# Feature-major products with high and low activations side by side as 512 moving columns, in groups of 512 outputs

## The chip, the cores and the metric

The kernel runs on one core of a Trainium2 chip. The metric is the device time of one execution in microseconds (us), given as the median of several runs. The profile is one further execution, taken by the hardware profiler; in it PE is TensorE's matmuls, PEld its weight loads, DVE VectorE, ACT ScalarE, POOL GpSimd, and SP the engine that issues nearly all DMAs.

## What is computed

A decoder trunk of two layers on one sequence of 256 tokens with 2048 features, in float32. Each layer is a token mixer and a gated MLP, each behind an RMSNorm that is shifted, scaled and gated by vectors made from a conditioning vector `c`:

```python
cond = silu(c)
for i in range(2):
    sh_m, sc_m, g_m, sh_f, sc_f, g_f = split(cond @ w_mod[i] + b_mod[i], 6)     # w_mod[i]: 2048 x 12288
    h = rmsnorm(x, norm_mix[i]) * (1 + sc_m) + sh_m
    y = gla_mixer(h, ...) if i == 0 else fox_mixer(h, ...)
    x = x + (1 + g_m) * y
    h = rmsnorm(x, norm_ffn[i]) * (1 + sc_f) + sh_f
    u = causal_depthwise_conv3(h @ w_up[i]) + conv_b[i]                         # w_up[i]: 2048 x 11264
    x = x + (1 + g_f) * ((silu(u[:, :5632]) * u[:, 5632:]) @ w_down[i])         # w_down[i]: 5632 x 2048
out = rmsnorm(x, norm_final)
```

The first mixer is chunked gated linear attention (input product 2048 x 6160 for q, k, v, a gate r and a rank-16 forget gate a; output product 2048 x 2048). The second is softmax attention with a cumulative forget-gate bias (input product 2048 x 8208 for q, k, v, an output gate and 16 forget logits; output product 2048 x 2048).

## The kernel before

**Numbers.** The large products are float32 products made of three fp32r matmuls. A weight tile `w` (128 rows by 1024 columns) is split into `wh` (a cast to fp32r on ACT, L110) and `wl = w - wh` (a subtraction on DVE, L111). The activations are split in the same way into a high part `rh` and a low part `rl`, which lie in one SBUF tile of shape [128, 2, 4, 256] (high and low parts of four row tiles). The product is wh·rh + wh·rl + wl·rh; the fourth term is left out.

**Streaming.** All weights pass once through the core, in the order of one list, `plan`: 816 tiles of 128 x 1024 (512 KB each) and three narrow ones. `next_w` loads them into a ring of five SBUF buffers (`RING`) and splits them up to three tiles ahead (`AHEAD`); the split halves have four buffers each. The same ring also holds the tiles `wm` of `w_mod`: the modulation vectors are background work, one 128 x 1024 tile at a time, multiplied by a column of silu(c) and added up on DVE (`acc`, L248). `tick`, called after each weight tile, loads and runs this background work and a queue of small steps (`side`: convolution, attention, operand preparation) at rates set by hand for each stage (`pace`, `set_pace`).

**Feature-major products, `stream_a`.** A weight tile gives eight output tiles of 128 features by 256 tokens (m = 0 to 7). For each, three matmuls with 256 moving columns are issued: wh with rh (L540), wh with rl (L541), wl with rh (L542), each with its own weight load. Four PSUM banks hold the eight outputs, two to a bank, and each row tile k of the contraction is added on. PSUM has eight banks: a pool `psA` of six (`PS[0]`), from which each product takes four, so that two are free when the next product begins, and a pool `psM` of two for all small work. The same pool serves the transposes that finish the modulation vectors (`pt`, L261) when they are wide or deferred.

The products of this form are: q, k and r of the linear attention (in two halves of the contraction, `BLOCKS`), its output product, both MLPs, and the output gate and the output product of the second mixer: 688 of the 816 tiles. The v product of the first mixer and the q, k, v of the second are token-major (`stream_b`, L573 to L575): there the activations are the loaded weights and 512 columns of the weight matrix move; 128 tiles.

**After a product.** An up-product's four banks are copied to SBUF by ACT (L1061 in `drain_psum`); four steps of convolution and activation follow in `side`. In the first MLP six groups of 1024 outputs are first multiplied with half the contraction, while the modulation vectors of the other half are still being made; the second half is then added on DVE (L1081). The output gate of the second mixer goes straight from PSUM through a tanh on ACT (L1023). An output or down product is scaled by the gate vector and added to the residual `xT` by one DVE instruction per output tile (L596 in `residual`); ACT squares the new residual (L394), and the sums of squares lead to the next RMSNorm. In the last product of each sub-layer the final `TAIL` = 3 row tiles are multiplied output by output, so that each pair of outputs is finished early.

**Between sub-layers.** `make_h` turns the sums of squares into a scale per token (`token_rstd`, on DVE), spreads it over the partitions with PE, and makes the activations row tile by row tile: L460 (DVE), L461 (ACT, high part), L462 and L463 (DVE, low part).

**Order.** The instructions of every engine are put in order by a scheduler that simulates the timeline, with program order as the priority; an engine then runs its own list strictly in that order.

## Time and profile before

| | |
|---|---|
| median of 3 runs | 2565.41 us (2563.37 to 2567.39) |
| profiled execution: span | 2570.5 us, 47584 instructions |
| PE busy, matmuls | 2515.7 us, 19242 |
| DVE busy | 1912.2 us |
| ACT busy | 1280.2 us |
| DMA | 638.36 MB, 248 GB/s over the span |
| granted TensorE clock, mean | 0.985 |

The span runs from the first to the last instruction of the profiled execution; it is 5.1 us above the median of the runs. Matmuls overlap in the record, and their ends are modelled, so PE's busy time is an upper picture: how fast PE really goes is read from the distance between the starts of matmuls. "Chain that ended last" is the work followed back from the last instruction, at each step to what released it, and says for each stretch of time which engine or transfer set the pace. In the tables by stretch, each engine's column is its busy time with its number of instructions, then the granted clock, the mean busy share of the 16 DMA engines, and the rate in GB/s.

### The profile page before, as it was taken

What the parts mean: (1) busy time and instruction counts of PE and PEld (TensorE: products, weight loads), DVE (VectorE), ACT (ScalarE), POOL (GpSimd) and SP (SyncE); (2) the same over time, 40 slices, a digit from 0 to 9 for tenths busy, and PEclk for the clock granted to TensorE, in tenths of its full rate; (3) what the DMA queues carried; (4) which work ended last, traced back from release to release, by engine and by line L of the source; (5) the groups of instructions that cost most, each with busy time, mean ns of one, the idle gap of its engine ahead of it and who ended that gap; (6) DMA issues with size and microseconds to landing.
All of it is one profiled execution on the core that took longest, in us unless ns stands there. A gap on an engine that the chain in (4) does not pass through costs nothing.

```text
span 2570.5 us, 47584 instructions
## 1 busy us (share of the span) xinstructions
PE 2515.7 (98%) x19242; PEld 2431.0 (95%) x19242; DVE 1912.2 (74%) x2570; ACT 1280.2 (50%) x1956; POOL 14.6 (1%) x35
## 2 busy tenths in 40 slices
PE   6999999999999999999999999999999999999998
PEld 6988899899999999999988889999999999999998
DVE  7767988876679998877587888777766667666544
ACT  2446454445555656543454555444545555565332
POOL 0000000000000000000000000000000000000000
PEclk7999999999999999999999999999999999999999
DMA  8897978798668888889489887686777767756553
GB/s 337 282 301 226 304 245 285 261 321 299 182 183 272 296 295 286 277 310 309 153 285 311 299 265 238 227 278 202 220 223 215 222 212 229 221 183 204 181 181 115
DMA packets 184313, 638.36 MB, mean 248 GB/s; under 512 B 23961, under 2 KB 24971, under 8 KB 183708
## 3 DMA queue, kind: packets, MB, share of 16 engines
q1 hardware_dynamic: 183704, 635.17, 74.9%
q8 instruction: 150, 2.46, 0.4%
q14 instruction: 71, 0.58, 0.1%
q10 hardware_dynamic: 388, 0.15, 0.0%
HBM read 633.14 MB, written 2.10 MB: 247 GB/s over the span
## 4 chain that ended last, share of the span: by engine, by line
PE 85%; DMA 7%; DVE 4%; issue 2%; ACT 1%; DVEq 0%; SPq 0%; ACTq 0%
PE pa L542 23%; PE pa L541 23%; PE pa L540 23%; DMA wm<-in_w_mod_dram 5%; PE pa L574 4%; PE pa L573 4%; PE pa L575 4%; DVE wl L111 2%; DVE acc L248 1%; DMA w<-in_ffn_w_down_dram 1%; DMA w<-in_gla_w_out_dram 1%; ACT wh L110 1%; PE pm L261 1%; DMA w<-in_gla_w_in_dram 0%; PE pm L777 0%
## 5 line engine op out<-in xcount | busy, mean ns | idle before, releaser
L110 ACT CAST wh<-w 128x1024 fp32r<-128x1024 f32 x819 | 855.1, 1047 | 1138.2 <-PE pa L541 677.6
L111 DVE TENSOR_TENSOR wl<-w,wh 128x1024 fp32r<-128x1024 f32 x819 | 995.6, 1219 | 455.7 <-ACT wh L110 444.6
L540 PE MATMUL pa<-h,wh 128*128 128x256 f32 x3584 | 1012.6, 285 | 5.6 <-ACT h L461 5.6
L542 PE MATMUL pa<-h,wl 128*128 128x256 f32 x3584 | 1015.0, 285 | 2.6 <-DVE wl L111 2.6
L541 PE MATMUL pa<-h,wh 128*128 128x256 f32 x3584 | 1015.8, 284 | 1.0 <-DVE h L463 0.9
L540 PEld LDWEIGHTS pa<-h,wh 128*128 128x128 f32 x3584 | 688.0, 193 | 6.8 <-ACT h L461 6.5
L542 PEld LDWEIGHTS pa<-h,wl 128*128 128x128 f32 x3584 | 688.8, 193 | 5.8 <-DVE wl L111 3.3
L541 PEld LDWEIGHTS pa<-h,wh 128*128 128x128 f32 x3584 | 690.1, 193 | 1.7 <-DVE h L463 1.4
L541 PE MATMUL pa<-op,wh 128*128 128x256 f32 x1920 | 540.4, 284 | 1.9 <-DVE op L479 1.9
L540 PE MATMUL pa<-op,wh 128*128 128x256 f32 x1920 | 539.6, 284 | 1.9 <-ACT wh L110 1.6
L248 DVE SCALAR_TENSOR_TENSOR acc<-wm,cT,acc 128x1024 f32<-128x1024 f32 x352 | 450.8, 1281 | 110.0 <-DMA wm<-in_w_mod_dram 109.4
L542 PE MATMUL pa<-op,wl 128*128 128x256 f32 x1920 | 530.2, 284 | 0.1
L541 PEld LDWEIGHTS pa<-op,wh 128*128 128x128 f32 x1920 | 369.3, 192 | 2.1 <-DVE op L479 2.1
L540 PEld LDWEIGHTS pa<-op,wh 128*128 128x128 f32 x1920 | 368.5, 192 | 2.5 <-ACT wh L110 2.0
L542 PEld LDWEIGHTS pa<-op,wl 128*128 128x128 f32 x1920 | 363.1, 192 | 0.7 <-DVE wl L111 0.7
L574 PE MATMUL pa<-wh,h 128*128 128x512 f32 x512 | 201.1, 393 | 0.0
L573 PE MATMUL pa<-wh,h 128*128 128x512 f32 x512 | 199.5, 393 | 0.9 <-ACT wh L110 0.9
L575 PE MATMUL pa<-wl,h 128*128 128x512 f32 x512 | 193.1, 394 | 0.0
L573 PEld LDWEIGHTS pa<-wh,h 128*128 128x128 f32 x512 | 96.6, 189 | 20.8 <-ACT wh L110 1.3
L574 PEld LDWEIGHTS pa<-wh,h 128*128 128x128 f32 x512 | 96.5, 189 | 19.8 <-issue 0.2
L575 PEld LDWEIGHTS pa<-wl,h 128*128 128x128 f32 x512 | 96.2, 189 | 19.1
L1039 ACT ACTIVATE y<-u,cw 128x256 f32<-128x256 f32 x176 | 101.6, 599 | 4.8 <-DVE act L1055 2.4
(236 smaller groups left out, 1389.9 us busy)
## 6 DMA issues: line engine op xcount, KB each, us to landing
wm<-in_w_mod_dram SPq DMA_DIRECT2D x352, 512.0 KB, 5.0
w<-in_ffn_w_up_dram SPq DMA_DIRECT2D x320, 512.0 KB, 4.3
w<-in_ffn_w_down_dram SPq DMA_DIRECT2D x176, 512.0 KB, 4.5
w<-in_fox_w_in_dram SPq DMA_DIRECT2D x128, 512.0 KB, 5.0
w<-in_gla_w_in_dram SPq DMA_DIRECT2D x96, 512.0 KB, 5.1
wm<-in_w_mod_dram SPq DMA_DIRECT2D x16, 1024.0 KB, 12.3
w<-in_gla_w_out_dram SPq DMA_DIRECT2D x32, 512.0 KB, 5.6
w<-in_ffn_w_up_dram SPq DMA_DIRECT2D x64, 256.0 KB, 3.9
```

What stands on the lines that cost most here:

```text
L110: nc.scalar.copy(out=hi, in_=src)
L111: order["v"] = nc.vector.tensor_tensor(out=lo, in0=src, in1=hi.bitcast(F32), op=ALU.subtract).ins
L248: nc.vector.scalar_tensor_tensor(out=st["a"], in0=wt[:, j, :], scalar=col, in1=st["a"], op0=ALU.mult, op1=ALU.add)
L261: nc.tensor.transpose(pt[:, m * P:(m + 1) * P], st["a"][:, (q0 + m) * P:(q0 + m + 1) * P], ident)
L540: nc.tensor.matmul(o, wh[:, ms], rh, start=(first and m % 2 == 0), stop=False, skip_group_check=True)
L541: nc.tensor.matmul(o, wh[:, ms], rl, start=False, stop=False, skip_group_check=True)
L542: nc.tensor.matmul(o, wl[:, ms], rh, start=False, stop=last, skip_group_check=True)
L573: nc.tensor.matmul(o, lh[:, ts_], wh[:, hs_], start=first, stop=False)
L574: nc.tensor.matmul(o, ll[:, ts_], wh[:, hs_], start=False, stop=False)
L575: nc.tensor.matmul(o, lh[:, ts_], wl[:, hs_], start=False, stop=last)
L1039: nc.scalar.activation(y, u, AF.Identity, scale=cw[:, l * 3 + 2, r:r + 1], bias=cw[:, 6 + l, r:r + 1])
```

## The change

`stream_a` is replaced by `stream_p`. Its products come in groups of 512 outputs (four output tiles) instead of 1024. A weight tile of 512 KB now holds two row tiles of 512 columns (`plan_pairs`), loaded by one DMA whose runs in memory are 2 KB instead of 4 KB; 688 tiles remain 688. For each output tile and row tile there are two matmuls: wh with the high and low activations side by side (512 moving columns, filling one PSUM bank: half the bank for wh·rh, half for wh·rl), and wl with the high activations (256 columns) added to the first half.

`psA` becomes three tiles of two banks, of which a group takes two. After a product the two halves of each bank have to be added: `gather` copies the second half with ACT (or, where a half contraction is added, adds it with DVE) and adds the first half with DVE. `residual` takes two DVE instructions per output tile instead of one. The gate's tanh follows a `gather`. The tail of a sub-layer's last product is two weight tiles (four row tiles) instead of three row tiles, for four output tiles instead of eight. The transposes and sums of the last norm are moved to fit (`prepare_out` queues three steps instead of two). `stream_b` and `narrow` keep their matmuls and take the new tiles.

The core of the diff:

```diff
-TAIL = 3
+TAIL = 2
-PS = (6, 2)
+PS = (3, 2)
+    def bank2(s="pa"):
+        return psA.tile([P, 2, 512], F32, tag="a", name=nm(s))
+    def plan_pairs(w, kts, c0):
+        kts = list(kts)
+        for kt in kts[::2]:
+            plan.append((w, kt, 2, ((c0, 512),)))
+                    if nk_ == 2:
+                        with after_startup():
+                            nc.sync.dma_start(out=wt.rearrange("p (k r) -> p k r", k=2),
+                                              in_=w_[kt_ * P:(kt_ + 2) * P, c0:c0 + cn]
+                                              .rearrange("(k p) r -> p k r", p=P))
+                        o = 2 * cn
-    def stream_a(kts, cols, rhs, done=None):
+    def stream_p(kts, c0, rhs, done=None):
+        ps = [bank2().rearrange("p j (s t) -> p j s t", s=2) for _ in range(2)]
         held = []
-        def mms(m, k, wh, wl, rh, rl):
+        def mms(m, k, ws, j, hl):
             first, last = k == kts[0], k == kts[-1]
-            ms = slice(m * P, (m + 1) * P)
-            o = ps[m // 2][:, m % 2, :]
-            nc.tensor.matmul(o, wh[:, ms], rh, start=(first and m % 2 == 0), stop=False, skip_group_check=True)
-            nc.tensor.matmul(o, wh[:, ms], rl, start=False, stop=False, skip_group_check=True)
-            nc.tensor.matmul(o, wl[:, ms], rh, start=False, stop=last, skip_group_check=True)
+            ms = slice(j * 512 + m * P, j * 512 + (m + 1) * P)
+            o = ps[m // 2][:, m % 2, :, :]
+            nc.tensor.matmul(o, ws[0][:, ms], hl, start=first, stop=False, skip_group_check=True)
+            nc.tensor.matmul(o[:, 0, :], ws[1][:, ms], hl[:, 0, :], start=False, stop=last, skip_group_check=True)
...
+    def gather(dst, ps, add=False):
+        if add:
+            nc.vector.tensor_tensor(out=dst, in0=dst, in1=ps[:, :, 1, :], op=ALU.add)
+        else:
+            nc.scalar.copy(out=dst, in_=ps[:, :, 1, :])
+        nc.vector.tensor_tensor(out=dst, in0=dst, in1=ps[:, :, 0, :], op=ALU.add)
...
-    def residual(l, key, m0):
+    def residual(l, key, m0, end):
         def done(pair, ps):
-            for j in range(2):
-                m = m0 + 2 * pair + j
-                nc.vector.scalar_tensor_tensor(out=xT[:, m, :], in0=ps[pair][:, j, :], scalar=modcol(l, key, m),
-                                               in1=xT[:, m, :], op0=ALU.mult, op1=ALU.add)
-            stat(m0 + 2 * pair, m0 > 0)
-            if fin and m0 and 0 < pair < 3:
-                transpose_out(m0 + 2 * pair - 2, 2)
+            for s_ in (1, 0):
+                for j in range(2):
+                    m = m0 + 2 * pair + j
+                    nc.vector.scalar_tensor_tensor(out=xT[:, m, :], in0=ps[:, j, s_, :], scalar=modcol(l, key, m),
+                                                   in1=xT[:, m, :], op0=ALU.mult, op1=ALU.add)
+            stat(m0 + 2 * pair, end)
         return done
...
+        def up(g, half, kts, add=False):
+            if half == 0 and not add:
+                us[g] = bigt([P, 8, T], "u")
+            ps = stream_p(kts, half * DFF + g * 512, h)
+            for b in range(2):
+                m = half * 4 + 2 * b
+                gather(us[g][:, m:m + 2, :], ps[b], add)
```

223 lines of the change are left out of this document (118 added, 105 removed).

## The prediction

> **What bounds the kernel now.** I read the head of the page first, then, for stretches between the sub-layers' ends, the shares of the chain that ended last, then the busy time of the engines there.
>
> ```profile
> span 2570.5 us, 47584 instructions
> PE 2515.7 (98%) x19242; PEld 2431.0 (95%) x19242; DVE 1912.2 (74%) x2570; ACT 1280.2 (50%) x1956; POOL 14.6 (1%) x35
> ```
>
> PE at 98% alone proves little, since matmul ends are modelled. The chain decides. Its shares follow in order of time, for 96 to 206 us (first half of the linear mixer), 206 to 500 (its rest and its output product), 500 to 1056 (first MLP, up product), 1056 to 1140 and 1140 to 1266 (its down product), 1566 to 1780 (attention's gate and output product), 1800 to 2550 (second MLP).
>
> ```profile
> by line: DMA wm<-in_w_mod_dram 53.5%; DVE wl L111 15.3%; issue 9.0%; DVE acc L248 5.2%; DMA w<-in_gla_w_in_dram 4.6%; PE pa L542 3.6%; PE pa L541 3.4%; PE pa L540 3.4%; PE pm L261 1.8%; DVEq L111 0.2%; DVEq L248 0.2%; DVE w L516 0.1%; DVE m
> by line: PE pa L542 13.7%; PE pa L540 13.7%; PE pa L541 13.7%; DMA w<-in_gla_w_out_dram 7.7%; DVE acc L248 4.6%; PE pa L573 4.6%; PE pa L574 4.6%; PE pa L575 4.6%; DMA wm<-in_w_mod_dram 4.4%; issue 3.7%; DVE wl L111 3.4%; PE pm L777 2.6%; P
> by line: PE pa L541 32.9%; PE pa L542 32.8%; PE pa L540 32.7%; PE pm L261 0.8%; DVE acc L248 0.2%; DVE wl L111 0.2%; ACT wh L110 0.2%; DVE op L479 0.1%; DVE hn L462 0.1%; issue 0.1%; DVE h L463 0.1%
> by line: DMA w<-in_ffn_w_down_dram 35.7%; DMA wm<-in_w_mod_dram 29.4%; DVE wl L111 13.4%; issue 8.5%; ACT wh L110 6.2%; DVE acc L248 3.5%; ACT pm L270 2.6%; DVE act L1055 0.5%; DVE y L1042 0.5%; ACTq L110 0.2%; DVEq L248 0.1%; DVEq L111 0.1
> by line: PE pa L540 33.4%; PE pa L541 33.1%; PE pa L542 33.0%; DVE xT L596 0.4%; issue 0.3%
> by line: PE pa L540 28.7%; PE pa L541 28.6%; PE pa L542 28.6%; PE pm L987 2.4%; PE pm L932 1.6%; PE pm L951 1.6%; PE pm L978 1.6%; PE pm L950 1.6%; PE pm L948 1.4%; PE pm L988 1.2%; PE pm L949 0.7%; PE pa L574 0.5%; PE pa L575 0.5%; PE pa L
> by line: PE pa L540 33.2%; PE pa L541 33.2%; PE pa L542 33.2%; PE pm L1112 0.2%; PE pm L261 0.2%
> ```
>
> In the third and the last three, nearly all of the chain is matmuls, three quarters or more of it the three lines that the change touches. A shorter matmul stream is a shorter span there. In the first and the fourth, the loop of a ring buffer (DMA, cast, subtraction, next DMA) sets the pace. The second is mixed.
>
> How long is one matmul on that path? The timeline gives starts. Between the first two rows lie 87 matmuls with 256 columns, between the last two 27 with 512.
>
> ```profile
> 1899.90 0.28 PE L540 MATMUL pa<-h,wh 128*128 128x256 f32 x1
> ...
> 1910.34 0.28 PE L540 MATMUL pa<-h,wh 128*128 128x256 f32 x1
> 1343.23 0.39 PE L573 MATMUL pa<-wh,h 128*128 128x512 f32 x1
> ...
> 1349.35 0.39 PE L573 MATMUL pa<-wh,h 128*128 128x512 f32 x1
> ```
>
> 10.44 / 87 = 120.0 ns and 6.12 / 27 = 226.7 ns. The 256 extra columns cost 106.7 ns, so a column costs 0.417 ns, and 13.3 ns are left per matmul at either width: a fixed price of each matmul with its weight load. The Trainium skill (TensorE: Matmul & The Clock Gate, section "Back-to-back issue gap") gives a gap of N/2.4 plus about 2.5 ns; this trace disagrees, with 13.3. By that rule the removed matmuls would be worth 5504 x 2.5 ns = 13.8 us at most.
>
> **The change, part by part: matmuls.** Columns stay: 3 x 256 = 512 + 256. One matmul in three goes.
>
> ```profile
> L540 PE MATMUL pa<-h,wh 128*128 128x256 f32 x3584 | 1012.6, 285 | 5.6 <-ACT h L461 5.6
> L540 PE MATMUL pa<-op,wh 128*128 128x256 f32 x1920 | 539.6, 284 | 1.9 <-ACT wh L110 1.6 <-DVE xT L596 0.3
> L111 DVE TENSOR_TENSOR wl<-w,wh 128x1024 fp32r<-128x1024 f32 x816 | 994.3, 1222 | 454.6 <-ACT wh L110 443.5 <-DMA w<-in_ffn_w_up_dram 4.0 <-PE pa L575 1.4
> L1061 ACT COPY u<-pa 128x512 f32<-128x512 f32 x88 | 50.7, 582 | 0.8
> L1081 DVE TENSOR_TENSOR u<-u,pa 128x512 f32<-128x512 f32 x24 | 15.4, 682 | 3.4 <-PE pa L542 3.3
> L596 DVE SCALAR_TENSOR_TENSOR xT<-pa,mod,xT 128x256 f32<-128x256 f32 x64 | 27.2, 477 | 13.9 <-PE pa L542 13.9
> ```
>
> 3584 + 1920 = 5504 triples, eight to a weight tile: 688 tiles. A triple goes from 360 to 226.7 + 120 = 346.7 ns, a tile from 2.88 to 2.773 us. The ceiling is 5504 x 13.3 ns = 73.4 us. How much arrives is read per stretch:
>
> ```profile
> 500.00:640.00 140.00, 140.00 (x1162) 139.91 (x1160) 104.61 (x109) 67.88 (x108) 0.00 (x0) 0.99 0.90 308
> 640.00:780.00 140.00, 139.96 (x1166) 139.84 (x1166) 105.73 (x156) 77.31 (x104) 0.00 (x0) 1.00 0.62 182
> 780.00:1010.00 230.00, 230.00 (x1921) 230.00 (x1921) 206.60 (x272) 134.09 (x220) 0.00 (x0) 1.00 0.86 293
> 950.00:994.00 44.00, 44.00 (x369) 44.00 (x368) 39.15 (x49) 24.18 (x33) 0.00 (x0) 1.00 0.86 293
> 1800.00:2270.00 470.00, 470.00 (x3920) 470.00 (x3920) 323.11 (x414) 253.79 (x366) 0.00 (x0) 1.00 0.70 218
> ```
>
> The fourth column is DVE. `gather` adds one DVE instruction per two output tiles; the nearest row is L1081, which also adds a PSUM bank: 682 ns. A whole group of 512 outputs is eight weight tiles and two extra instructions, 0.171 us a tile; a half contraction has four tiles, 0.341 us a tile, in both its passes.
> - Second MLP (264 tiles), attention's gates (32) and output product (32): DVE in the second MLP goes from 323.11/470 x 2.88 = 1.98 to 2.15 us of 2.773, 78%. Full saving: 328 x 0.107 = 35.0 us.
> - First MLP, half contractions, 96 tiles: DVE goes from 75% to about 2.50 of 2.773, 90%; in the row of 780 to 1010 us PE is busy throughout beside a DVE at 90%. Full: 10.2 us.
> - First MLP, the other 80 up tiles: DVE is at 206.60/230 = 90% now, 2.59 us a tile; with 0.17 more it needs 2.76 of 2.773, 99.5%, and no row here has it over 90%. Busy at 96.5%, about midway, it would take 2.86 us a tile: of 8.5 us I take 80 x 0.02, 1.5.
> - First MLP, down: 84 us (29 tiles) hang on the buffer loop and give nothing; 59 tiles give 6.3 us.
> - Linear mixer with its output product, 96 tiles, ceiling 10.2 us: chain on DMA, or mixed. I take 2.
>
> Together 55.0 us.
>
> **Transfers.** Each stays one issue of 512 KB, in runs of 2 KB instead of 4. The last up group loads such runs already, in pieces of 256 KB:
>
> ```profile
> w<-in_ffn_w_up_dram SPq DMA_DIRECT2D x31, 256.0 KB, 4.2
> ```
>
> This is 950 to 994 us: 293 GB/s at a share of 0.86, as in 780 to 1010, which is mostly 4 KB runs. So the runs cost nothing, SP's queue keeps its count, and casts and subtractions keep theirs.
>
> **Draining a group.** This is the new wait. Before, a pool of six banks left two free, and a bank needed one ACT copy (582 ns). Now one tile of two banks is free; the next group's outputs 2 and 3 need the tile that the old group's outputs 0 and 1 fill. From their last matmul to that need lie two outputs of the old and two of the new group, 8 x 346.7 ns = 2.77 us. In it must fit the copy and, behind it, the DVE add: 0.58 + 0.68 = 1.26 us, and whatever DVE is running: a subtraction (1.22 us) ahead fits with 0.3 us to spare, a second one doesn't. After an output product two bank pairs cost four L596 instructions, 1.9 us. Behind a late add, the next subtraction waits on DVE, and PE behind that. There are 16 + 4 groups in the linear mixer, 38 and 26 in the two MLPs, 4 + 4 at attention's end: 92, of which 72 where PE sets the pace. The cost per group is between 0 and one more DVE instruction, 1.2 us; the wait that fits is nearer, so 0.2 us: 14.4 us (0 to 86; a gain is excluded, since no drain gets shorter).
>
> **Ends of sub-layers.** At the last pair PE is idle and everything waits for L596:
>
> ```profile
> 1780.34 0.88 DVE L596 SCALAR_TENSOR_TENSOR xT<-pa,mod,xT 128x256 f32<-128x256 f32 x2 [1.14 <-PE pa L542]
> 1788.57 0.58 ACT L461 ACTIVATE h<-hn,mod 128x256 fp32r<-128x256 f32 x1
> 1789.21 1.22 PE L540 MATMUL pa<-h,wh 128*128 128x256 f32 x4 [2.63 <-ACT h L461]
> 1789.64 0.43 DVE L463 TENSOR_TENSOR h<-hn,h 128x256 fp32r<-128x256 f32 x1
> 1791.38 0.42 DVE L463 TENSOR_TENSOR h<-hn,h 128x256 fp32r<-128x256 f32 x1
> ```
>
> Two instructions become four: 0.88 us more, at four ends 3.5 us. At the next start PE now begins with the high part at 1789.21; a 512-wide matmul needs the low part too, at 1790.07, 0.9 us later, and row tile 1 (1791.80) soon after. I take 1.2 us at three starts, 3.6 us (0 to 2.6 each, the second row). The wide and deferred `pt` transposes, which had six banks, now share three tiles; a four-block read takes 4 x (254 + 182) ns:
>
> ```profile
> L270 ACT ACTIVATE pt<-pt 128x128 f32<-128x128 f32 x32 | 8.1, 254 | 0.0
> L270 ACT ACTIVATION_READ_ACCUMULATOR pt<-pt 128x1 f32 x32 | 5.8, 182 | 0.0
> ```
>
> That is 1.74 us per wait at startup and two sub-layer starts, but ACT reads one block after another anyway, so I take 0.5 each, 1.5. The shorter tail and the moved output transposes have cover from PE and cost nothing. Ends: 8.6 us.
>
> **Sum.** 55.0 - 14.4 - 8.6 = 32 us off the span, 2570.5 to 2538.5. The span is 5.1 us above the median of the runs; against that median I forecast 2533 us, with 2505 (draining free, half the ends, some gain on the mixer: 60 us) to 2558 (groups at 0.55 us) as this case's own range. Over 0.2% (5 us) is what a measurement of this kernel can tell from no change.
>
> **The rivals.**
> - Slower: DVE becomes the bound through the drains. At the end of each group its two adds stand behind two long instructions instead of one, the tile comes free 1.2 us late, and the subtraction of a later weight tile is pushed back too. Price 72 x 1.2 = 86 us: 55.0 - 8.6 - 86 = -40, 2605 us. It decides from 46.4/72 = 0.64 us per group on. For it: 90% DVE in 780 to 1010, and one free tile instead of two free banks. Against: 68% in the second MLP, where 26 groups lie, and a scheduler that can put later matmuls on the free tile first. 0.16.
> - No change: two smaller limits together where DMA is at 0.86 and more. The buffer loop holds its old pace in the first passes and the rest of the up product too, 46 us instead of 55, and drains cost 0.5 us: 46 - 36 - 8.6 = 1, 2564 us. For it: share 0.90 at 308 GB/s in 500 to 640. Against: no DMA in that stretch's chain. 0.09.
> - The saving isn't there: the 13.3 ns turn up again, because the load behind a pair's second, short matmul is the one that is not covered. Only costs remain: 14.4 + 8.6 = 23, 2588 us. Against: 106.7 ns for 256 more columns is the same 0.417 ns that leaves 13.3 at both widths. 0.05. The Trainium skill's 2.5 ns (same page and section) would leave 55.0 x 2.5 / 13.3 = 10 us of saving, 2578 us, near this rival and within its chance.
>
> **Numbers.** The forecast has 0.70, the others 0.16, 0.09 and 0.05. Faster 0.72 (the forecast and the upper end of the second), same 0.06, slower 0.22. Range 2505 to 2580: it takes in the no-change case and the mild end of the others and leaves out about 0.05 below and 0.15 above.
>
> **What would show it.** Starts of wide and narrow matmuls alternating at 226.7 and 120 ns; 2.773 us a weight tile from 1800 us on; DVE over 95% in the second part of the first MLP's up product with PE waiting there for `wl`; PE waits for the first add of `gather` short and few; L596 four times at each end. If PE's idle time before matmuls, by releaser, stands at 40 us or more on `gather` and its followers, the first rival holds; if the pair takes 360 ns, the third does.

## The result, and the profile after

The changed kernel takes 2594.32 us (median of 4 runs, 2590.81 to 2598.36), the kernel before in the same session 2566.19 (2563.37 to 2567.39). The ratio is 1.0112 (95% interval 1.0098 to 1.0127): about 29 us slower, where 32 us less were forecast. The profiled execution took 2593.84 us, 1.7 of them outside its span.

The head of the page of the changed kernel, and its chain that ended last, by engine and by line:

```profile
span 2592.1 us, 36814 instructions
...
PE 2486.6 (96%) x13738; PEld 2139.2 (83%) x13738; DVE 2010.2 (78%) x2784; ACT 1288.2 (50%) x1964; POOL 18.1 (1%) x35
...
PE 72%; DVE 12%; DMA 10%; issue 3%; ACT 3%; DVEq 0%; SPq 0%; ACTq 0%
PE pa L554 38%; PE pa L555 19%; DMA wm<-in_w_mod_dram 7%; DVE wl L111 4%; PE pa L601 4%; PE pa L599 4%; PE pa L600 4%; DVE acc L252 3%; ACT wh L110 1%; DVE xT L624 1%; DMA w<-in_ffn_w_down_dram 1%; DMA w<-in_gla_w_in_dram 1%; DMA w<-in_ffn_
```

The chain of the kernel before, by engine:

```profile
PE 85%; DMA 7%; DVE 4%; issue 2%; ACT 1%; DVEq 0%; SPq 0%; ACTq 0%
```

TensorE has 29 us less busy time, VectorE 98 us more, and the span is 21.6 us longer all the same. The chain shows where it went: before, 85% of it was TensorE and 4% VectorE. Now it is 72% and 12%, and DMA's share goes from 7% to 10%. In more places than before, something other than matmuls sets the pace.

The stretches that the forecast used, for the changed kernel (stretch, then its length, PE, PEld, DVE, ACT, POOL busy with counts, granted clock, DMA share, GB/s): the DVE-limited part of the first MLP's up product, and the steady part of the second MLP.

```profile
806.00:1034.00 228.00, 226.53 (x1297) 196.98 (x1296) 215.34 (x292) 138.38 (x234) 0.00 (x0) 1.00 0.88 299
1900.00:2250.00 350.00, 350.00 (x2005) 305.12 (x2004) 258.10 (x341) 192.83 (x266) 0.00 (x0) 1.00 0.72 226
```

In the second row 2005 instructions take 350.00 us. Eight of them are transposes of 0.1 us, so a pair takes 2 x 349.2 / 1997 = 349.7 ns, where three matmuls took 360 before. A pair saves 10.3 ns and not 13.3: in this stretch of the timeline the next matmul starts 232 ns after a long one and 117 ns after a short one (medians), where 226.7 and 120 were forecast. In the first row VectorE is busy 94% of the time and the transfers run at 299 GB/s.

Where the time went by part of the program, read off the timelines (before: 61.31, 496.88, 1265.65, 1789.21, 2555.73 us; after: 61.99, 514.02, 1283.14, 1824.38, 2575.64). The first, second and fourth time are the start of a part's first product matmul. The third and the fifth are the start of a down product's last matmul by L540 (L554 in the changed kernel), so the norm behind the first MLP is counted to attention. The columns on the right are experiments told below.

| part, us | before | after | e3 | e7 | e6 | e14 | e15 | e9 |
|---|---|---|---|---|---|---|---|---|
| linear mixer and its output product | 435.6 | 452.0 | 439.7 | 461.0 | 435.5 | 432.1 | 450.7 | 451.5 |
| first MLP | 768.8 | 769.1 | 773.2 | 782.3 | 755.2 | 770.1 | 759.1 | 768.6 |
| attention and its output product | 523.6 | 541.2 | 525.5 | 531.0 | 530.2 | 540.4 | 531.6 | 525.9 |
| second MLP | 766.5 | 751.3 | 771.2 | 772.6 | 755.9 | 753.1 | 757.6 | 766.4 |

Only the second MLP became faster. The linear mixer lost 16 us and attention 18. Each column is one profile. In the one of before the span lies 5 us above the median of the runs, and with the 1.7 us outside the span that the changed kernel shows, that execution was some 7 us over the median (an estimate). So differences of a few us to that column are not safe, and the losses may be larger by 7 us in all.

What TensorE waited for, in the waits by releaser (us in all, times, longest), changed kernel:

```profile
PE pa L554 <- DVE op L483: 14.8, 4, 7.3
PE pa L555 <- DVE wl L111: 10.8, 9, 3.0
...
PE pa L554 <- DVE h L467: 7.8, 4, 4.3
...
PE pa L554 <- DVE xT L624: 2.9, 4, 0.8
...
PE pa L554 <- DVE u L585: 1.2, 3, 0.5
```

and the rows of the same kind before:

```profile
PE pa L542 <- DVE wl L111: 2.6, 3, 1.2
...
PE pa L541 <- DVE op L479: 1.9, 1, 1.9
...
PE pa L541 <- DVE h L463: 0.9, 1, 0.9
```

The waits for the drains themselves (`xT` L624 and `u` L585) are small, 4.1 us in all, with 0.7 more for the other tiles that L585 writes (`r` and `thf`). What grew is the waiting for operands that VectorE makes: `op`, `wl` and the low part of `h`, in these rows from 5.4 to 33.4 us. The largest single one is at the start of the first MLP's down product (start, duration, engine, line; idle time in brackets):

```profile
1036.98 0.28 PE L555 MATMUL pa<-op,wl 128*128 128x256 f32 x1
1037.72 0.47 DVE L1082 SCALAR_TENSOR_TENSOR y<-u,cw,y 128x255 f32<-128x255 f32 x1
...
1038.11 1.21 DVE L111 TENSOR_TENSOR wl<-w,wh 128x1024 fp32r<-128x1024 f32 x1
...
1039.25 0.47 DVE L1084 SCALAR_TENSOR_TENSOR y<-u,cw,y 128x254 f32<-128x254 f32 x1
...
1040.09 4.25 ACT L482 CAST op<-act 128x512 fp32r<-128x512 f32 x8
1040.33 1.28 DVE L252 SCALAR_TENSOR_TENSOR acc<-wm,cT,acc 128x1024 f32<-128x1024 f32 x1 [0.61 <-DMA wm<-in_w_mod_dram]
1041.53 0.48 DVE L1084 SCALAR_TENSOR_TENSOR y<-u,cw,y 128x254 f32<-128x254 f32 x1
1041.92 1.22 DVE L111 TENSOR_TENSOR wl<-w,wh 128x1024 fp32r<-128x1024 f32 x1
1043.06 0.48 DVE L1082 SCALAR_TENSOR_TENSOR y<-u,cw,y 128x255 f32<-128x255 f32 x1
...
1043.45 0.42 DVE L1097 TENSOR_TENSOR act<-u,y 128x256 f32<-128x256 f32 x1
1043.79 1.29 DVE L483 TENSOR_TENSOR op<-act,op 128x512 fp32r<-128x512 f32 x2
...
1044.53 0.79 PE L554 MATMUL pa<-op,wh 128*128 128x512 f32 x1 [7.26 <-DVE op L483]
...
1045.33 0.63 PE L554 MATMUL pa<-op,wh 128*128 128x512 f32 x1
...
1045.97 0.63 PE L554 MATMUL pa<-op,wh 128*128 128x512 f32 x1
```

TensorE stops at 1037.3 us and starts again at 1044.53. VectorE is never idle for long in between: subtractions of weights (L111), modulation (L252) and the convolution that is left over from the up product (L1082, L1084, L1097) all come before the subtraction that makes the operand (L483).

### The profile page after: what moved, and what is told of

It reads as the page before. It is cut to its first block, busy times and chain, and to the rows that moved or that the text cites. A ratio compares the mean times of both kernels' runs of the same rounds, so it can differ in the third digit from the quotient of the medians.

```text
span 2592.1 us, 36814 instructions
## 1 busy us (share of the span) xinstructions
PE 2486.6 (96%) x13738; PEld 2139.2 (83%) x13738; DVE 2010.2 (78%) x2784; ACT 1288.2 (50%) x1964; POOL 18.1 (1%) x35
## 4 chain that ended last, share of the span: by engine, by line
PE 72%; DVE 12%; DMA 10%; issue 3%; ACT 3%; DVEq 0%; SPq 0%; ACTq 0%
PE pa L554 38%; PE pa L555 19%; DMA wm<-in_w_mod_dram 7%; DVE wl L111 4%; PE pa L601 4%; PE pa L599 4%; PE pa L600 4%; DVE acc L252 3%; ACT wh L110 1%; DVE xT L624 1%; DMA w<-in_ffn_w_down_dram 1%; DMA w<-in_gla_w_in_dram 1%; DMA w<-in_ffn_w_up_dram 0%; PE pm L411 0%; PE pm L265 0%
## 5 line engine op out<-in xcount | busy, mean ns | idle before, releaser
L111 DVE TENSOR_TENSOR wl<-w,wh 128x1024 fp32r<-128x1024 f32 x819 | 994.4, 1218 | 368.0 <-ACT wh L110 361.4
L554 PE MATMUL pa<-h,wh 128*128 128x512 f32 x3584 | 1264.4, 399 | 15.9 <-DVE h L467 7.8
L555 PE MATMUL pa<-h,wl 128*128 128x256 f32 x3584 | 992.8, 282 | 6.7 <-DVE wl L111 6.6
L554 PEld LDWEIGHTS pa<-h,wh 128*128 128x128 f32 x3584 | 671.4, 189 | 169.3 <-ACT h L465 8.1
L555 PEld LDWEIGHTS pa<-h,wl 128*128 128x128 f32 x3584 | 681.9, 190 | 21.9 <-DVE wl L111 9.4
L554 PE MATMUL pa<-op,wh 128*128 128x512 f32 x1920 | 676.0, 398 | 18.9 <-DVE op L483 14.8
L555 PE MATMUL pa<-op,wl 128*128 128x256 f32 x1920 | 531.9, 281 | 4.2 <-DVE wl L111 4.2
L252 DVE SCALAR_TENSOR_TENSOR acc<-wm,cT,acc 128x1024 f32<-128x1024 f32 x352 | 450.7, 1280 | 104.9 <-DMA wm<-in_w_mod_dram 103.9
L554 PEld LDWEIGHTS pa<-op,wh 128*128 128x128 f32 x1920 | 359.8, 189 | 103.6 <-DVE op L483 15.2
L555 PEld LDWEIGHTS pa<-op,wl 128*128 128x128 f32 x1920 | 363.9, 190 | 9.5 <-DVE wl L111 6.0
L601 PEld LDWEIGHTS pa<-wl,h 128*128 128x128 f32 x512 | 96.5, 189 | 20.1 <-DVE wl L111 0.4
L600 PEld LDWEIGHTS pa<-wh,h 128*128 128x128 f32 x512 | 96.5, 189 | 19.2
L1082 DVE SCALAR_TENSOR_TENSOR y<-u,cw,y 128x255 f32<-128x255 f32 x176 | 84.0, 477 | 0.0
L1084 DVE SCALAR_TENSOR_TENSOR y<-u,cw,y 128x254 f32<-128x254 f32 x176 | 82.6, 476 | 0.7
L585 DVE TENSOR_TENSOR u<-u,pa 128x512 f32<-128x512 f32 x112 | 75.7, 679 | 4.0 <-ACT u L584 3.9
L624 DVE SCALAR_TENSOR_TENSOR xT<-pa,mod,xT 128x256 f32<-128x256 f32 x128 | 53.1, 476 | 20.1 <-PE pa L555 20.1
```

Source lines behind the costliest of these rows:

```text
L111: order["v"] = nc.vector.tensor_tensor(out=lo, in0=src, in1=hi.bitcast(F32), op=ALU.subtract).ins
L252: nc.vector.scalar_tensor_tensor(out=st["a"], in0=wt[:, j, :], scalar=col, in1=st["a"], op0=ALU.mult, op1=ALU.add)
L554: nc.tensor.matmul(o, ws[0][:, ms], hl, start=first, stop=False, skip_group_check=True)
L555: nc.tensor.matmul(o[:, 0, :], ws[1][:, ms], hl[:, 0, :], start=False, stop=last, skip_group_check=True)
L600: nc.tensor.matmul(o, ll[:, ts_], wh[:, hs_], start=False, stop=False)
L601: nc.tensor.matmul(o, lh[:, ts_], wl[:, hs_], start=False, stop=last)
```

## The experiments

Three things came with the change: groups of 512 outputs in place of 1024, a second read of every bank, and two matmuls in place of three. The experiments first took them apart, then looked for the place of each. Differences in us between whole runs are worked out from the ratios to the kernel before, times 2566.

### First theories: fresh operands at a doubled rate (T), or draining (D)

**e3_narrow_256.** One part of the change alone: the groups of 512.

```diff
-            nc.tensor.matmul(o, ws[0][:, ms], hl, start=first, ...)
+            nc.tensor.matmul(o[:, 0, :], ws[0][:, ms], hl[:, 0, :], start=first, ...)
+            nc.tensor.matmul(o[:, 0, :], ws[0][:, ms], hl[:, 1, :], start=False, ...)
             nc.tensor.matmul(o[:, 0, :], ws[1][:, ms], hl[:, 0, :], ...)
...
-            for s_ in (1, 0):
+            for s_ in (0,):
```

> One part of the change alone: groups of 512 outputs, but three 256-column matmuls per block into one half of the bank, so one read drains a tile and VectorE has no addition more than in the kernel before. TensorE's matmul time is that of the kernel before (2465 us), 73 us over the changed kernel's. Theory T: a group still goes through the contraction twice as fast as in the kernel before, so nearly all of the 93 us of new waiting stays apart from what the slower matmuls hide: 2625 to 2650. Rival D (draining the two halves is the cost): the waiting goes away with the second read, and the time falls to that of the kernel before, 2565 to 2590.

Measured: 2587.02 us, ratio 1.0087 (1.0072 to 1.0102), 22 us over the kernel before. That is in the rival's range. Theory T on its own is wrong: the narrower groups cost something, but not the 60 to 80 us that would have explained everything.

**e1_wide_first.** The first 1024 outputs over each fresh operand in the old form, with a 1024-wide weight tile.

```diff
-        for g in range(3):
+        ps = stream_w(kts, [(0, 1024)], rhs)   # three 256-column matmuls per block
+        ...
+        for g in (2,):
             ps = stream_p(kts, g * 512, rhs)
```

> The changed kernel, but the first 1024 outputs over each freshly made operand (the linear mixer's query columns, the first 1024 outputs of every output product and of every down product, the first up group and its gate half) run in the old form: 1024 outputs at once, three 256-column matmuls per block, high and low in one accumulator. 168 of the 688 weight tiles are in the old form. Theory T (a narrow group goes through the contraction twice as fast, so that a fresh operand is wanted at twice the rate and TensorE waits for VectorE): the holes at the starts go back to their old size, about 33 us less lost (linear output product 9, second down 12, the two halves of the first up 4, and the other starts 8), for 18 us more of matmul time (168 tiles x 8 outputs x 13.3 ns): 2560 to 2585, about 15 us or more under the changed kernel's 2594. Rival D (the time goes into draining: two reads and one addition more per tile, spread over all groups): only a quarter of the drains go back, and the matmul time is lost: 2600 to 2612.

Measured: 2566.01 us, ratio 1.0002 (0.9993 to 1.0012), 28 us under the changed kernel although 18 us of matmul time were given up by the forecast's 13.3 ns a pair (14 by the 10.3 ns measured above). The starts over fresh operands are a place where the time is lost, as T said. The waits of e1 by releaser agree (us in all, times, longest):

```profile
PE pa L555 <- DVE wl L111: 6.9, 4, 3.3
...
PE pa L590 <- DVE op L483: 2.6, 2, 1.9
...
PE pa L590 <- DVE h L467: 1.7, 1, 1.7
```

For `op` 14.8 us have become 2.6, for the low part of `h` 7.8 have become 1.7. A part of it has moved to the high parts, which ACT makes and which the old form needs first: the waits of these products for them go from 2.8 to 9.0 us. But e1 gives back the wide groups and the single read at once, so it cannot tell which of them matters there.

**e4_no_low.** VectorE's work on fresh operands cut.

```diff
-            nc.vector.tensor_scalar(out=t, in0=t, scalar1=sc, scalar2=sh, ...)
-            ins = nc.vector.tensor_tensor(out=lo, in0=t, in1=hi.bitcast(F32), op=ALU.subtract).ins
+            nc.gpsimd.memset(lo.bitcast(F32), 0.0)
...
-                nc.vector.tensor_tensor(out=lo, in0=src, in1=hi.bitcast(F32), op=ALU.subtract)
+                nc.gpsimd.memset(lo.bitcast(F32), 0.0)
```

> The changed kernel with the low part of the activations left out: it is set to zero by GpSimd, and two VectorE operations per row tile in the normalised operand and one per pair of row tiles in the raw operands are gone; every matmul and every drain stays. Theory T: with VectorE quicker at making fresh operands the holes at the starts shrink: 2550 to 2575. Rival D (drains): the drains are unchanged, 2585 to 2595.

Measured: 2564.26 us, ratio 0.9991 (0.9976 to 1.0007), 31 us less than the changed kernel. VectorE is busy 75 us less than in the changed kernel (1935.2 us). Matmuls, groups and drains are the changed kernel's, so the waits hang on VectorE's work on operands, and not on the drains by themselves as rival D had it. Whether it is the load, or the wait for the low part itself (which is zero here, and so ready early), this run can't tell apart. Nor does it tell what of the change has loaded VectorE too much, the rate or the second read.

**e2_gate_drain.** The call that empties the side queue, one group later.

```diff
-                if g == 1 and hf == 0:
+                if g == 1 and hf == 1:
                     drain_side()
```

> The changed kernel with the call that empties the queue of side work moved from the first to the second half of the gates' second weight group, one group of 16 weight-tile uses later, so that the attention heads that are left can be put between more matmuls. Theory T2 (the hole of 15 us at 1686 to 1702 is side work emptied eight steps earlier than in the kernel before): 8 to 13 us faster than the changed kernel, 2581 to 2586, and the hole shrinks. Rival (the hole is the attention chain's own length, and only moves): no change, 2592 to 2597.

Measured: 2588.14 us, ratio 1.0093 (1.0074 to 1.0112), 5 us less, half of what was expected. In the place itself all of it is there. The changed kernel's timeline, TensorE alone, shows heads with waits between them from 1686 to 1701.60, and the row of that stretch TensorE at 16.70 of 22 us:

```profile
1689.04 0.42 PE L1017 MATMUL pm<-ident,s 128*128 128x128 f32 x1 [2.59 <-DVE s L1006]
...
1694.73 1.19 PE L1026 MATMUL pm<-pt,v 128*128 128x256 f32 x2 [0.29 <-DVE s L994]
...
1698.59 0.30 PE L1017 MATMUL pm<-ident,s 128*128 128x128 f32 x1 [1.00 <-DVE s L1006]
...
1700.38 0.70 PE L1026 MATMUL pm<-pt,v 128*128 128x256 f32 x2 [0.62 <-ACT pt L1019]
...
1701.60 0.50 PE L554 MATMUL pa<-h,wh 128*128 128x512 f32 x1 [0.29 <-DVE thf L585]
```

```profile
1680.00:1702.00 22.00, 16.70 (x72) 12.64 (x73) 11.94 (x31) 10.04 (x31) 1.13 (x2) 0.84 0.57 144
```

In e2 the corresponding stretch is full:

```profile
1660.00:1710.00 50.00, 49.33 (x282) 41.99 (x281) 44.05 (x69) 28.48 (x53) 6.54 (x4) 1.00 0.87 234
```

The gates (first to last group) go from 129.5 to 119.2 us. The output product behind them takes 108.5 instead of 105.9, the rest of the 10 us is not found in one place.

### The square: second read by matmul length

**e7_two_reads_256.** e3 with the second read put back. The low activations go to the other half of the bank.

```diff
+            nc.tensor.matmul(o[:, 0, :], ws[0][:, ms], hl[:, 0, :], start=first, ...)
+            nc.tensor.matmul(o[:, 1, :], ws[0][:, ms], hl[:, 1, :], start=False, ...)
             nc.tensor.matmul(o[:, 0, :], ws[1][:, ms], hl[:, 0, :], ...)
```

> Groups of 512 outputs with three 256-column matmuls as in e3 (TensorE's time as before the change), but the low activations' product goes to the other half of the bank, so that every bank is read twice as in the changed kernel: the second read without the shorter matmuls. Theory J (joint): some slack of VectorE is used up, but the longer weight tiles cover most of it: 10 to 30 us over e3, 2597 to 2617. Rival W (what costs is the wait for a bank, and it costs the same at any length of a matmul, 80 us over e3's): 2650 to 2670. Rival T (the second read has no part in it): 2585 to 2592, as e3.

Measured: 2625.97 us, ratio 1.0231 (1.0216 to 1.0247), 37 us over e3.

**e6_one_read.** The changed kernel without the second read.

```diff
-            nc.scalar.copy(out=dst, in_=ps[:, :, 1, :])
-        nc.vector.tensor_tensor(out=dst, in0=dst, in1=ps[:, :, 0, :], op=ALU.add)
+            nc.scalar.copy(out=dst, in_=ps[:, :, 0, :])
...
-            for s_ in (1, 0):
+            for s_ in (0,):
```

> The changed kernel with the second read of each bank left out: only the high activations' half is read (one ACT copy, or one VectorE addition where a sum is continued, and one residual instruction per output tile), so the product of the low activations is computed by TensorE but doesn't reach the result. Matmuls, groups and order stay; VectorE has about 100 us less. With the three 256-column matmuls (e3, one read, 2587) and the changed kernel (512 columns, two reads, 2594) this is the third corner of a square. Theory J (joint: TensorE waits because VectorE's second read comes on top of shorter weight tiles and fresh operands; neither alone does it): most of the 73 us arrive once the read is gone, 2525 to 2550. Rival T (the doubled rate at which a narrow group wants a fresh operand, with no part for the second read): the holes at the starts stay, 2575 to 2590.

Measured: 2557.69 us, ratio 0.9972 (0.9959 to 0.9986), 7 us under the kernel before and 36 under the changed kernel.

Neither theory J nor T gave either number. The square is simpler than both:

| over the kernel before, us | three matmuls of 256 | 512 and 256 | shorter matmuls |
|---|---|---|---|
| one read | e3: +22.3 | e6: -7.2 | -29.5 |
| two reads | e7: +59.3 | after: +28.7 | -30.6 |
| second read | +37.0 | +35.9 | |

The effects add, to within 1 us, well inside the intervals (each reaches 3 to 4 us to either side). So there are three prices: narrower groups 22, second read 36, shorter matmuls -30; the sum is 28. The chain of 208 to 500 us (second half of the linear mixer, and its output product) shows the second read at work; first e3, then e7:

```profile
by line: PE pa L554 17.2%; PE pa L555 17.0%; PE pa L556 17.0%; PE pa L600 4.4%; PE pa L599 4.4%; PE pa L601 4.3%; DMA wm<-in_w_mod_dram 4.0%; DMA w<-in_gla_w_out_dram 3.7%; issue 3.4%; DVE acc L252 3.3%; DVE wl L111 2.8%; PE pm L816 1.9%; P
```

```profile
by line: DMA wm<-in_w_mod_dram 21.9%; DVE wl L111 13.0%; DVE acc L252 9.3%; issue 9.1%; DMA w<-in_gla_w_in_dram 8.7%; ACT wh L110 4.3%; PE pa L555 4.1%; PE pa L554 4.0%; PE pa L556 3.9%; DVE xT L625 2.0%; DMA w<-in_gla_w_out_dram 2.0%; ACT 
```

With one read half of the chain is the three matmul lines, not far from the kernel before (41% in the prediction's row for 206 to 500 us). With two reads it is mostly the buffers' loop: DMA, cast, subtraction, modulation.

**e9_before_dve.** VectorE's extra work without anything else of the change.

```diff
-                nc.scalar.copy(out=u[:, 2 * b:2 * b + 2, :], in_=ps[b])
+                d_ = u[:, 2 * b:2 * b + 2, :]
+                nc.scalar.copy(out=d_, in_=ps[b])
+                nc.vector.tensor_tensor(out=d_, in0=d_, in1=d_, op=ALU.max)
```

> The kernel before, with the VectorE work of the second read put in as idle work: behind each read of a feature-major product VectorE takes the maximum of the result with itself, 512 or 256 columns, with no change of value. About 90 us more of VectorE, wide groups and 256-column matmuls stay. Theory J: wide groups and longer weight tiles hide it: 2566 to 2580. Rival V (VectorE is so near to the bound that its work counts almost in full wherever it is put): 2600 to 2650.

Measured: 2592.23 us, ratio 1.0104 (1.0087 to 1.0121), 27 us over the kernel before, between the two theories. VectorE is busy 104 us more (2016.3 us), about as much as the second read adds (107 us between e6 and the changed kernel). The table by parts tells more than the total: 15.9 us are lost in the linear mixer, 2.3 in attention, and nothing in the two MLPs. (By spans the loss is 19 us, because the profile of before lies above its median; where the other 8 us belong is not known.) What TensorE waits for in the linear mixer is not the weights here: its waits for `wl` fall from 2.6 to 1.2 us, and those for two tiles of the norms, `dg` and `ss`, go from 2.8 to 12.8.

### The place of the second read

**e14_one_read_mixer** and **e15_one_read_rest.** `gather` and `residual` with a switch, so that the second read is left out in the linear mixer and its output product only, or everywhere else only.

```diff
-            for s_ in (1, 0):
+            for s_ in ((0,) if ((l, key) == (0, "g_m")) == True else (1, 0)):   # e15: == False
```

> The changed kernel with the second read of the banks left out in the linear mixer's query, key and gate columns and in its output product only (20 of the 92 groups, 96 of the 688 weight tiles), so that there the low activations' product doesn't reach the result. Theory V (VectorE is part of the loop that frees weight buffers there, so its extra work counts nearly in full): 14 to 22 us less than the changed kernel, about half of the 36 that the second read costs in all: 2572 to 2580. Rival D (each group costs about the same): 20/92 of 36, 8 us, 2584 to 2588. By the forecast's own terms: 0, 2592 to 2596.

> The opposite: the second read is left out everywhere but in the linear mixer and its output product. Theory V: 14 to 22 us less than the changed kernel, 2572 to 2580. Rival D: 72/92 of 36, 28 us, 2564 to 2568. By the forecast's own terms: 14 us, and no more, 2578 to 2582.

Measured: e14 2575.95 us, ratio 1.0038 (1.0027 to 1.0050), 19 us less than the changed kernel; e15 2577.24 us, ratio 1.0044 (1.0028 to 1.0060), 17 us less. Together 36, the whole price. Both are in theory V's range, and outside rival D's. In e14 the gain is where it should be: 452.0 to 432.1 in the first row of the table, within 1.8 us elsewhere. So 20 groups pay 0.95 us each, the other 72 only 0.24 on average. By VectorE's busy time, 26 us of work less gives 19 us in the one place, 81 us less gives 17 in all the others. That average hides much: in e15's column the first MLP gains 10.0 us and attention 9.6, but the second MLP, with 26 of the 72 groups, loses 6.3.

How the 20 us go in the linear mixer is seen in its row and its waits, first the changed kernel, then e14; the third row is e15, which keeps the second read here (columns as in the rows by stretch above).

```profile
61.99:514.02 452.03, 418.73 (x2348) 356.92 (x2349) 375.18 (x499) 215.82 (x349) 4.32 (x10) 0.95 0.79 262
62.04:494.13 432.09, 412.02 (x2348) 351.53 (x2349) 349.92 (x451) 216.36 (x349) 4.32 (x10) 0.98 0.82 274
62.17:512.90 450.73, 417.32 (x2348) 356.35 (x2349) 374.99 (x499) 215.97 (x349) 4.32 (x10) 0.96 0.79 263
```

```profile
PE pa L555 <- DVE wl L111: 8.6, 5, 3.0
PE pa L554 <- DVE op L483: 6.5, 2, 5.7
PE pm L369 <- DVE dg L367: 6.2, 3, 2.8
```

```profile
PE pa L554 <- DVE op L483: 4.0, 1, 4.0
PE pa L555 <- DVE wl L111: 3.2, 4, 1.3
...
PE pm L369 <- DVE dg L367: 2.9, 1, 2.9
```

TensorE is idle 13 us less, and its busy time is 7 us shorter for the same matmuls: the granted clock is 0.98 in place of 0.95. The waits that shrink are mostly for what VectorE makes: the weights' low halves (`wl`), the operands (`op`), the norm (`dg`); a wait of 4.1 us for ACT's high part of `h` goes too. In e15 the waits for `wl`, `op` and `dg` are 8.7, 6.8 and 6.2 us, as in the changed kernel.

### The shorter matmuls: where a pair's 3 ns go

**e10_grouped.** Same matmuls, eight long ones and then eight short ones.

```diff
-            for m in range(4):
-                for j in range(2):
-                    mms(m, k0 + j, ws, j, hls[j])
+            for part in range(2):
+                for j in range(2):
+                    for m in range(4):
+                        mms(m, k0 + j, ws, j, hls[j], (part,))
```

> The changed kernel with another order of the same matmuls: within a weight tile first the eight 512-column matmuls, then the eight 256-column ones, instead of one after the other in turn (the last two weight tiles of an output product's last group keep the old order). In the changed kernel a clean pair takes 349.5 ns on average, not the 346.7 that 226.7 and 120.0 make, so 10.5 ns are saved per pair and not 13.3. Theory P (the turn from long to short and back is what costs the 3 ns): the pitches settle at 226.7 and 120.0, and 10 to 16 us go: 2578 to 2586. Rival (the 3 ns belong to the 512-column matmul beside the VectorE and ScalarE work, whatever its neighbour): the mean pair stays at 349 to 351 ns, 2588 to 2597. The subtraction that makes the low weights is also wanted 1.8 us later within a tile, which could take off a few us of waits for it under either.

Measured: 2601.23 us, ratio 1.0139 (1.0120 to 1.0157); beside 1.0112 the intervals overlap, and the gain that theory P expected isn't there. The timeline gives the pitches (x8: eight in a row):

```profile
1951.15 2.00 PE L555 MATMUL pa<-h,wh 128*128 128x512 f32 x8
1952.99 1.11 PE L557 MATMUL pa<-h,wl 128*128 128x256 f32 x8
1953.94 2.00 PE L555 MATMUL pa<-h,wh 128*128 128x512 f32 x8
```

Eight long ones take 1952.99 - 1951.15 = 1.84 us, 230 ns each, eight short ones 0.95 us, 119 ns each. Over all of 1900 to 2250 us the mean is 232 and 119. The turn from long to short is not the cause: it is the long matmul that takes 230 to 232 instead of 226.7.

**e12_contiguous.** The two parts of an operand side by side in memory.

```diff
-                st["t"] = big.tile([P, 2, 4, T], F32R, tag="s8", ...)
+                st["t"] = big.tile([P, 4, 2, T], F32R, tag="s8", ...)
```

> The changed kernel with the high and low activations of one row tile side by side in memory (the buffer is laid out as 4 row tiles x 2 parts instead of 2 parts x 4 row tiles), so that the 512 moving columns are one run; in the changed kernel they are two runs of 256, 4 KB apart. In e10, where 512-column matmuls follow one another, they start 231.6 ns apart on average, but the linear mixer's value columns, one run of 512, 227.4. Theory L (the second run costs the 4 ns): the mean pair falls from 349.5 to 347.5 or less, 5504 x 2 to 3 ns = 11 to 16 us if TensorE sets the pace there, 2578 to 2584. Rival (the layout has no part in it): the pair stays at 349 to 351 and the time at 2590 to 2598.

Measured: 2592.08 us, ratio 1.0106 (1.0093 to 1.0119). The steady part of the second MLP:

```profile
1900.00:2250.00 350.00, 350.00 (x2006) 305.12 (x2005) 259.28 (x342) 192.39 (x264) 0.00 (x0) 1.00 0.71 226
```

2006 instructions where the changed kernel had 2005. The layout has no part in it. The cause of the 3 ns stays open.

### Versions that keep the good part

**e8_select** (new form only in places that gained) and **e11_second_mlp** (new form only in the last 80 weight tiles of the first up product and in the second MLP).

```diff
+            ps = stream_w(kts, [(c0, 1024)], h)        # linear mixer, gates, output products: old form
...
+        for g in range(n_first, NG):                   # e11: stream_p from here on only
```

> The new form only where the changed kernel spent less time than the kernel before: first MLP from its second pass on, its down product's second half, second MLP apart from its first up group; the old form (1024 outputs at once, three 256-column matmuls) in the linear mixer, the output products, the gates, the first pass of the first MLP and the first 1024 outputs of its down product. From the stages of the changed kernel and of e1: the rest of the first up product 5 to 7 us less than before, its second pass 2, second MLP's up product 11 to 13, its down product 2 to 4, and nothing elsewhere: 20 to 26 us under the kernel before, 2539 to 2546. If waits only move from one stage to the next (rival M), the gain is under 10 us: 2556 or more.

> The new form only in the last 80 weight tiles of the first MLP's up product and in the whole second MLP (up and down), the old form with 1024 outputs everywhere else, and the first MLP's first three pairs of groups taken with 1024 gate and 1024 value columns as in the kernel before. From the stages of e8 against the kernel before: rest of the first up product 5, second up product 12, its down product 3 us less, nothing elsewhere: 2543 to 2550. Rival M (each place's gain returns as a wait of the same size in the next place): 2555 to 2562, as e8 gave.

**e13_mlp_contiguous** is e11 with the layout of e12 (80 + 176 + 88 = 344 weight tiles are in the new form).

> e11 (new form only in the last 80 up tiles of the first MLP and in the second MLP; 2561) with the layout of e12. 344 - 88 + 88 = 344 weight tiles, 2752 pairs, are in the new form. Theory L: 2752 x 2 to 3 ns = 5 to 8 us less than e11, 2552 to 2556. Rival: 2558 to 2564.

Measured: e8 2559.23 us, ratio 0.9975 (0.9964 to 0.9985); e11 2561.09 us, 0.9978 (0.9969 to 0.9988); e13 2561.32 us, 0.9987 (0.9978 to 0.9996). All three beat both kernels, but by 3 to 6 us and not by 15 to 25. In e11's profile the places in the new form gained what was expected (rest of the first up product 233.0 to 226.7, second MLP 766.5 to 753.2), and parts in the old form took 8 us more than in the one profile of before (linear mixer 440.6 instead of 435.6), which lies above its median besides. In e8's profile the second MLP takes 751.0 us, and the linear mixer (436.0), the first MLP (769.4) and attention (524.4) stay within 1 us of that profile: a gain of 13 us by spans, of 6 by medians. So rival M holds in the total; whether the waits really move, or two single profiles differ by that much, is not settled.

## Why the prediction was wrong, step by step

The sum had three terms, and the runs measured each:

| us | forecast | measured | by |
|---|---|---|---|
| shorter matmuls | -55.0 | -30 | e6 - e3, after - e7 |
| second read (draining 14.4, four ends 3.5) | +17.9 | +36 | e7 - e3, after - e6 |
| of it in the linear mixer and its output product | 0.9 (one end) | +19 | after - e14 |
| of it elsewhere | 17.0 | +17 | after - e15 |
| narrower groups (starts 3.6, `pt` 1.5) | +5.1 | +22 | e3 - before |

- **The step that failed first: "72 where PE sets the pace".** The second read was charged to the groups where TensorE is the bound, and the 20 groups of the linear mixer were left out, because the chain there hangs on DMA and the buffers' loop. That was the wrong way round. VectorE makes most of what TensorE waits for there, and the prediction itself has the subtraction among the steps of that loop. e14 measures the second read there at 19 us, where the forecast had 0.9; e9 finds 16 with nothing but idle VectorE work. That it costs so much there is shown. That it acts through the buffers' loop is not: the waits for `wl` are 5 of the 13 us of idle time that e14 wins, the rest is at operands and norms, and in e9 the waits for `wl` don't grow at all. The slower clock behind the idle times adds 7 us. "I take 2" for the saving on the mixer was low, but not the error: with one read (e6 against e3) the part saves 4.
- **The 0.2 us per group elsewhere came out by luck.** 17/72 = 0.24 is near it, but it is an average over places that differ: by e15's column the second read costs 10.0 us in the first MLP's 38 groups, 9.6 in attention's 8, and nothing in the second MLP's 26, where the changed kernel is 6.3 us faster than e15. Nor was it a wait for the drains, as it was reckoned: those are 5 us in the whole kernel.
- **Shorter matmuls: two errors.** First, 13.3 ns per removed matmul was taken from the pitch of two kinds of matmul and came out as 10.3 in the stream of pairs; 55.0 x 10.3 / 13.3 = 43. Second, the attention gates gave a loss instead of their 3.4 us: the working does not mention that the side queue is now emptied after 24 of the gates' 32 weight tiles. e6 loses 7 us at the gates against e3 (126.9 and 119.9), and e2 wins 10 there. 43 - 10 = 33, near the measured 30. Why e3, with the same call at the same place, has no hole is open. By parts of the table (e6 - e3, in brackets what was forecast) the pairs give -4.2 us in the linear mixer (-2), -18.0 in the first MLP (-18.0), +4.7 in attention (-6.8) and -15.3 in the second MLP (-28.2), where a pair of e6 takes 353 ns.
- **Narrower groups: the missing term.** The change was read as "Columns stay" and "One matmul in three goes". That a group of 512 outputs goes through the contraction in half the time, and asks for a fresh operand at twice the rate, is nowhere in the sum but for the three starts. e3 prices the groups of 512 at 22 us, with the smaller things that came along (three tiles of two banks, a shorter tail, moved drains, transfers in runs of 2 KB), against 5.1 for starts and `pt`. How the 22 divide among them was not tried, and that the doubled rate is the main part is not shown: e3's loss lies in all four parts of the table (4.1, 4.4, 1.9 and 4.7 us).
- **What held.** Transfers in runs of 2 KB cost no throughput (299 GB/s at a share of 0.88, before 293 at 0.86). The 80 tiles in the DVE-limited part took 228.3 / 80 = 2.85 us each (start of the first to start of the last long matmul), 2.86 forecast, with VectorE at 94% instead of 96.5. The second MLP gained 15.2 us; forecast were 264 x 0.107 - 26 x 0.2 = 23, and with 10.3 ns per pair it would have been 17.
- **The rivals.** The slower one (DVE becomes the bound through the drains, 2605 us) named the right engine. Its first mechanism, a tile that comes free 1.2 us late after every group, is not what happened: TensorE's waits on the drains are 5 us, far below the 40 that it set as its sign. Its second, that the subtraction of a later weight tile is pushed back, is a part of it: the waits for `wl` go from 2.6 to 10.8 us. Against it the forecast had set VectorE's 68% in the second MLP, and there the argument was right; it said nothing of the linear mixer. Nearest to the result lies the third rival (the saving isn't there, 2588 us), by luck: it needs a pair of 360 ns, and 349.7 were measured. The second (no change, 2564 us) named the first MLP's first passes, and they saved nothing (146.1 us, before 142.7), but with one read they take 141.3 (e6), so the buffer loop's old pace isn't the whole reason. Its sum is off a little too: the places that it names come to 6.6 us of the 55.0, and not 9.

The chain's shares by themselves would not have shown the second read's part. In the stretch of 208 to 500 us, the lines of the changed kernel, of e14 and of e15:

```profile
by line: PE pa L554 13.0%; DVE wl L111 11.9%; DMA wm<-in_w_mod_dram 10.2%; issue 9.4%; DVE acc L252 7.8%; PE pa L555 6.8%; DMA w<-in_gla_w_in_dram 5.6%; ACT wh L110 3.9%; DVE xT L624 2.7%; DMA w<-in_gla_w_out_dram 2.0%; DMA w<-in_ffn_w_up_d
```

```profile
by line: PE pa L554 19.2%; DMA wm<-in_w_mod_dram 11.2%; PE pa L555 9.4%; DVE wl L111 8.5%; issue 7.9%; DVE acc L252 7.4%; DMA w<-in_gla_w_out_dram 4.5%; DMA w<-in_gla_w_in_dram 3.7%; ACT wh L110 3.6%; DMA w<-in_ffn_w_up_dram 2.1%; PE pm L84
```

```profile
by line: PE pa L554 20.6%; PE pa L555 10.5%; DVE wl L111 9.1%; DVE acc L252 6.1%; PE pa L607 5.1%; PE pa L605 5.0%; PE pa L606 5.0%; issue 4.7%; DMA w<-in_gla_w_out_dram 4.2%; ACT wh L110 2.8%; PE pm L822 2.6%; PE pm L844 2.5%; DMA wm<-in_w
```

The share of the product's matmuls (L554, L555) goes from 20% to 29% in e14, and that of the subtraction from 12 to 8.5. But e15 has 31% and 9.1%, although it keeps the second read here and its part is as long as the changed kernel's (450.7 and 452.0 us). The times of the parts decide, not the shares of one chain. The same caution holds for the chains of e3 and e7 above.

## What to carry to other kernels

Where the chain hangs on a buffer's loop, list every engine that the loop passes through, and what else these engines make there: here work added to VectorE cost most in such a place (19 us for 26 us of work), and a saving on TensorE little (4 us). When a change cuts a group in half, ask what is now wanted at twice the rate, before counting what is saved in the steady state. And price the parts of a combined change apart: two corner kernels (one read, three matmuls) settled here in one run each what the profile of the whole left ambiguous.

## What the runs showed of the hardware

A hole in TensorE's stream costs more than its own length. Three stretches of the changed kernel around the hole at 1037 us, with the granted clock (third number from the end of a row):

```profile
1037.30:1040.50 3.20, 0.00 (x0) 0.00 (x0) 2.59 (x5) 1.36 (x2) 0.00 (x0) 1.00 0.90 292
1040.60:1047.40 6.80, 2.87 (x9) 2.49 (x10) 6.80 (x11) 3.74 (x8) 0.00 (x0) 0.50 0.88 317
1047.50:1055.00 7.50, 7.50 (x45) 6.57 (x45) 7.50 (x14) 4.84 (x7) 0.00 (x0) 1.00 0.31 84
```

TensorE's last matmul ends at 1037.3. The clock falls to half about 3.3 us later and stays there until 1047.4, 2.9 us after the matmuls are back; in the timeline above a pair then takes 1045.97 - 1045.33 = 0.64 us instead of 0.35. The Trainium skill (TensorE: Matmul & The Clock Gate, section "What's actually happening") gives half rate after an idle window of about 3.4 us, and full rate after as long a busy one; the trace comes near, with 3.3 and 2.9 us. Over the span the mean granted clock is 0.985 before, 0.975 in the changed kernel and 0.983 with one read (e6). Other holes show it too: the granted clock is 0.54 from 405 to 420 us and 0.72 from 1814 to 1832.

A long matmul over the high and low activations starts 230 to 232 ns after the one before it (e10), one with 512 columns of the weight matrix moving 226.7 ns (in the kernel before). It is neither the neighbour (e10) nor the layout (e12). It isn't constant between kernels either: in e6, 1991 instructions (16 of them transposes) fill the stretch from 1900 to 2250 us that holds 2005 in the changed kernel, which makes 353 ns a pair, and in e6 and e15, with one read there, the second MLP takes 5 to 6 us more than in the changed kernel. No run tells why.
